# Gate and up blocks: high and low token halves as one 512-column operand in two of three accumulators

## The chip, the cores and the metric

One core of one Trainium2 chip runs the whole program. The metric is the device time of one execution in microseconds (us). The engines are TensorE (PE: matmuls, with its weight loads listed apart as PEld), VectorE (DVE), ScalarE (ACT), GpSimd (POOL) and SyncE (SP), whose queue issues most of the DMAs. PE adds its results into accumulators in PSUM, eight banks of 512 float32 columns for each of 128 partitions; everything else is in SBUF.

## The reference, cut to what matters

Two layers of an encoder with 512 tokens and 1024 channels. Each layer has a token mixer (three branches, merged by gates), a feed-forward block (FFN) and an embedding block (ple). Only the FFN's first half and the hand-overs into and out of it are touched here:

```
x = x + merged @ w_o[i]
h = rmsnorm(x, norm_ffn[i])
x = x + (silu(h @ w_ffn_gate[i]) * (h @ w_ffn_up[i])) @ w_ffn_down[i]
h = rmsnorm(x, norm_ple[i])
x = x + sigmoid(h @ w_ple_gate[i]) * (p[i] @ w_ple_in[i])
```

The FFN is 2816 wide, which is 22 blocks of 128. All values are float32.

## The kernel before

**Float32 in parts.** PE is given a rounded form of float32 (fp32r in the rows), so each operand is kept as a high part and a low part (`split`: ACT copies the high part, DVE subtracts it to get the low part). A product is three matmuls: high weights with high tokens, high weights with low tokens, low weights with high tokens. Tokens are the columns that stream; weights (128 x 128) stand.

**Gate and up.** The FFN runs over 11 steps (`gate_up`), each with two blocks of gate and two of up weights. A step doesn't take the eight half-size products of a 2 x 2 block scheme but seven, with sums of weights and sums of the two token halves (256 tokens each) as operands. Their names are a11, a12, s1, s2, s3, s4, a22. `product` (L1141) does one: 4 chunks of the contraction (`kp`) x 2 outputs `u` (gate, up) x 3 matmuls of 256 columns = 24 matmuls. The order on PE in a step is a11, a12, s2, s1, s3, s4, a22; in a layer's first step it is a11, a12, s1, s2, s3, s4, a22, begun in parts.

Three accumulators take them, one bank each: x (name ffn_sc, two buffers) gets a11, s2, s3 and a22 one on top of the other; y (ffn_tr, two buffers) gets a12; z (ffn_av, one buffer) gets s1 and then s4 on top of it. With three banks for everything else (ffn_mm), that is all eight. After each product `after(name)` reads the accumulator: a11, s2, s1 and a22 by an ACT copy into a quarter of the output, a12, s3 and s4 by a DVE add onto one. The output is two tiles g, for two blocks: half 0 and half 1 of the tokens, each with gate and up. After s4 the first tile of the step is complete, after a22 the second. `mid` then makes the operand of the second half of the FFN from a tile: DVE multiplies the gate by the row factor of the norm (wo_r), ACT takes silu, DVE multiplies by up, ACT and DVE split into high and low half. Steps alternate between two sets of output tiles (ffn_pt in even steps, ffn_y in odd ones).

**Down.** After steps 0 to 3, 4 to 7 and 8 to 10 follows `down`: eight output blocks of 8, 8 and 6 mids, in matmuls of 512 columns (L177, L178, L179 for the three parts), accumulated in ffn_mm and added to x by DVE. The last two mids of a group come last in its first two blocks.

**Order.** PE's order is the order in which the program is written. Each item (a product or a `down` block) has its weights prepared three items ahead: for a product `parted`, ACT to ffn_wh and DVE to ffn_wl, 1024 columns, three buffers each; the sums s2 and s4 are made by DVE first (ffn_rp). Loads are issued by SP some items ahead into ffn_wr, ffn_e and ffn_kh (L1041, and L1154 for `down`); sums of two loaded matrices are accumulated by DMAs issued by POOL (L1043). On ACT and DVE a scheduler orders the instructions by priority and by what it believes of their times; `follow` ties a preparation behind the latest read of an accumulator (`mark`) on the same engine. All of ACT's copies and silus are recorded at L143, all of DVE's two-operand operations at L157.

**Into and out of the FFN.** While `w_o` runs, `halves_in` and `halves_out` make the seven token operands from each chunk of the normed x. The FFN's norm is done on the way: transposes of squares into ffn_tr banks, DVE sums them, POOL takes the power (column wo_rc), and transposes broadcast it (wo_tr). At the end of `ffn` the norm for ple is begun by `main_norm`.

Of the kernel before, what the change touches and what calls it, by code (L numbers as in the profile page):

```python
# [1 line left out]

# [10 lines left out]
F32R = mybir.dt.float32r  # L13
# [7 lines left out]
P = 128  # L21
# [40 lines left out]
class Net:  # L62
    def __init__(self, nc, tc, a):
# [12 lines left out]
        self.col = self.rb = self.xin = None  # L76

# [61 lines left out]
    def ps(self, tag, shape=(P, 512), dt=F32):  # L139
        return self.psum.tile(list(shape), dt, name=self.nm(tag), tag=tag, bufs=self.pbufs[tag])  # L140
# [65 lines left out]
    def norm(self, sq, n, waits, done, spread=True, eps=None):  # L206
# [4 lines left out]
        st = self.ps("tr", (P, 4, P))  # L211
# [12 lines left out]
        bc = self.ps("tr", (P, 4, P))  # L224
# [66 lines left out]
    def build(self):  # L291
# [4 lines left out]
        self.pbufs = dict(mm=3, sc=2, tr=2, av=1)  # L296
        with tc.tile_pool(name="sb", bufs=1) as self.pool, \
# [4 lines left out]
            with tc.manual_schedule(engines={mybir.EngineType.PE}):  # L302
                h = self.opening()
                xsrc = a["xT"]
                for i in range(L):
                    h = self.layer(i, h, xsrc, xs)
                    xsrc = xs

# [129 lines left out]
    def layer(self, i, h, xsrc, xs):  # L438
# [41 lines left out]
        x, h = self.w_o(mg, xsrc, extra)  # L480
        h = self.ffn(h, x, extra)
        return self.ple(h, x, xs, self.inputs() if i == L - 1 else None)
# [506 lines left out]
    def halves_in(self, kp, x):  # L989
# [3 lines left out]
        if kp == 2:  # L993
            big = [self.sb("qk", [P, 8, 256], F32R) for _ in range(2)]
            hi, lo = [[(b[:, 0:4], 0, 4), (b[:, 4:7], 4, 7)] for b in big]
        else:
            tag = "v" if kp == 3 else "h"
            four = [self.sb(tag, [P, 4, 256], F32R) for _ in range(4)]
            hi, lo = [[(b[0], 0, 4), (b[1][:, 0:3], 4, 7)] for b in (four[0:2], four[2:4])]
# [7 lines left out]
        out = [(h[:, j], l[:, j]) for (h, a, z), (l, _, _) in zip(hi, lo) for j in range(z - a)]  # L1007
        return dict(kp=kp, bases=bases, raw=raw, other=other, hi=hi, lo=lo, out=out)

    def halves_out(self, t, x):  # L1010
# [4 lines left out]
        self.act(raw[6], x[:, 256:], AF.Copy, scale=g)  # L1015
        self.stt(raw[2], raw[3], -1.0, raw[6], ALU.mult, ALU.subtract)
        self.tt(raw[4], raw[6], t["other"], ALU.subtract)
        self.stt(raw[5], raw[2], -1.0, raw[1], ALU.mult, ALU.subtract)
        for (h, a, z), (l, _, _), b in zip(t["hi"], t["lo"], t["bases"]):
            self.split(h, l, b[:, 0:z - a])  # L1020
# [9 lines left out]
    def gate_up(self, step, ts, mids, extra):  # L1030
# [32 lines left out]
        def run(bank, name, j, kps=range(KP), first=False):  # L1063
            if bank not in out:
                out[bank] = self.ps(dict(x="sc", y="tr", z="av")[bank], (P, 2, 256))
# [527 lines left out]
```

## Time and profile before

| | us |
|---|---|
| median of three runs | 1772.5 (1772.41 to 1774.06) |
| profiled execution | 1772.31 |
| its span in the profile | 1770.5 |

| engine | busy us | share of the span | instructions |
|---|---|---|---|
| PE | 1764.0 | 100% | 10017 |
| PEld | 1550.4 | 88% | 10017 |
| DVE | 1371.0 | 77% | 2111 |
| ACT | 898.3 | 51% | 1482 |
| POOL | 63.5 | 4% | 102 |

The granted PE clock stands at full in all 40 slices, and DMA moves 145 GB/s in the mean. In the profile, instructions are named by output and inputs, with the buffer's number left out: `ffn_sc<-wo_h,ffn_wh` adds token operand wo_h times high weights ffn_wh into accumulator x. Token operands are wo_h, wo_qk and wo_v by chunk. In a timeline the row is start, length (latency, not pitch), engine, line, operation, names and shapes; brackets at the end give idle time before it and what ended that. In the chain of waits a row is start, length, and the work on the path.

### The profile page before, as it was taken

The page shows a single profiled execution, that of the slowest core. Times are in us where ns is not written, and L with a number is a line of the kernel's source. Part 1 is how long each engine was busy: PE and PEld are TensorE (multiplying, and loading weights), DVE is VectorE, ACT ScalarE, POOL GpSimd, SP SyncE. Part 2 cuts the span into 40 slices and gives each one's busy share as a digit, 9 for nine tenths or more (in the row PEclk, how much of TensorE's full clock was granted, in tenths as well). Part 3 has the DMA queues.
Part 4 walks back from the last instruction along what each step waited for, and adds up shares of the span by engine and source line. Part 5 has one row for each costly group of instructions (what it writes and reads, how often), then busy time and mean ns, then how long its engine had stood idle before and what let it go on. Part 6 is the DMA issues. An engine that isn't in the chain of part 4 may idle for free.

```text
span 1770.5 us, 26539 instructions
## 1 busy us (share of the span) xinstructions
PE 1764.0 (100%) x10017; PEld 1550.4 (88%) x10017; DVE 1371.0 (77%) x2111; ACT 898.3 (51%) x1482; POOL 63.5 (4%) x102
## 2 busy tenths in 40 slices
PE   9999999999999999999999999999999999999998
PEld 7888888888899899898888888888888998998987
DVE  7689887997877577577796788869878775775776
ACT  5566556325665255255545665563356652542544
POOL 0000000000010000000000000000000100100000
PEclk9999999999999999999999999999999999999999
DMA  5666453335656366253537574423364762763432
GB/s 194 191 191 180 126 140 84 102 99 174 196 156 178 127 167 179 85 143 118 160 122 191 177 183 122 135 84 107 105 197 139 191 191 85 187 173 111 122 111 96
DMA packets 98672, 257.51 MB, mean 145 GB/s; under 512 B 12912, under 2 KB 18160, under 8 KB 98544
## 3 DMA queue, kind: packets, MB, share of 16 engines
q1 hardware_dynamic: 91200, 231.26, 42.0%
q0 software_dynamic: 6336, 23.07, 7.4%
q8 instruction: 79, 1.29, 0.3%
q10 hardware_dynamic: 1008, 1.48, 0.2%
q14 instruction: 49, 0.40, 0.1%
HBM read 216.44 MB, written 7.86 MB: 127 GB/s over the span
## 4 chain that ended last, share of the span: by engine, by line
PE 98%; DMA 1%; DVE 0%; ACT 0%; issue 0%; ACTq 0%
PE ffn_sc L1141 14%; PE ffn_av L1141 7%; PE ffn_mm L178 4%; PE ffn_mm L179 4%; PE ffn_mm L177 4%; PE ffn_tr L1141 4%; PE mergea_mm L179 2%; PE mergea_mm L177 2%; PE mergea_mm L178 2%; PE natten_mm L177 2%; PE diff_sc L847 2%; PE gatec_mm L178 2%; PE natten_mm L178 2%; PE diff_mm L177 2%; PE diff_mm L178 2%; PE natten_mm L179 2%
## 5 line engine op out<-in xcount | busy, mean ns | idle before, releaser
L143 ACT ACTIVATE ffn_wh<-ffn_wr 128x1024 fp32r<-128x1024 f32 (+1 forms) x114 | 116.6, 1028 | 193.3 <-PE ffn_mm L178 102.0
L160 DVE SCALAR_TENSOR_TENSOR conv_z<-glu_z,pre_par,conv_z 128x512 f32<-128x512 f32 x240 | 179.2, 747 | 3.0
L157 DVE TENSOR_TENSOR ffn_wl<-ffn_wr,ffn_wh 128x1024 fp32r<-128x1024 f32 (+1 forms) x114 | 135.1, 1185 | 53.3 <-ACT ffn_wh L143 52.8
L1141 PE MATMUL ffn_sc<-wo_h,ffn_wh 128*128 128x256 f32 x704 | 130.4, 283 | 0.0
L1141 PEld LDWEIGHTS ffn_sc<-wo_h,ffn_wh 128*128 128x128 f32 x704 | 110.4, 192 | 0.8
L1141 PE MATMUL ffn_sc<-wo_h,ffn_wl 128*128 128x256 f32 x352 | 99.6, 283 | 0.0
L177 PE MATMUL ffn_mm<-ffn_z,ffn_wh 128*128 128x512 f32 x240 | 93.4, 389 | 0.0
L178 PE MATMUL ffn_mm<-ffn_z,ffn_wh 128*128 128x512 f32 x240 | 93.4, 389 | 0.0
L179 PE MATMUL ffn_mm<-ffn_z,ffn_wl 128*128 128x512 f32 x240 | 93.4, 389 | 0.0
L157 DVE TENSOR_TENSOR ffn_t<-ffn_mm,wo_r 128x512 f32<-128x512 f32 x48 | 33.1, 690 | 69.2 <-PE ffn_mm L179 69.2
L157 DVE TENSOR_TENSOR ffn_wl<-ffn_rp,ffn_wh 128x1024 fp32r<-128x1024 f32 x44 | 53.8, 1223 | 30.1 <-ACT ffn_wh L143 30.1
L143 ACT ACTIVATE mergea_wh<-mergea_wr 128x1024 fp32r<-128x1024 f32 (+1 forms) x32 | 27.1, 847 | 88.8 <-PE mergea_mm L178 80.4
L1141 PEld LDWEIGHTS ffn_sc<-wo_h,ffn_wl 128*128 128x128 f32 x352 | 67.5, 192 | 0.0
L1141 PE MATMUL ffn_sc<-wo_qk,ffn_wh 128*128 128x256 f32 x352 | 67.1, 283 | 0.0
L1141 PE MATMUL ffn_sc<-wo_v,ffn_wh 128*128 128x256 f32 x352 | 67.1, 283 | 0.0
L1141 PE MATMUL ffn_av<-wo_h,ffn_wh 128*128 128x256 f32 x352 | 65.3, 283 | 0.0
L143 ACT ACTIVATE ffn_wh<-ffn_rp 128x1024 fp32r<-128x1024 f32 x44 | 46.4, 1055 | 29.4 <-PE ffn_mm L178 17.5
L1141 PEld LDWEIGHTS ffn_sc<-wo_qk,ffn_wh 128*128 128x128 f32 x352 | 54.9, 192 | 0.0
L1141 PEld LDWEIGHTS ffn_av<-wo_h,ffn_wh 128*128 128x128 f32 x352 | 54.9, 192 | 0.0
L1141 PEld LDWEIGHTS ffn_sc<-wo_v,ffn_wh 128*128 128x128 f32 x352 | 54.9, 192 | 0.0
L179 PEld LDWEIGHTS ffn_mm<-ffn_z,ffn_wl 128*128 128x128 f32 x240 | 45.1, 188 | 9.4
L946 DVE TENSOR_REDUCE diff_s<-diff_sc 128x1 f32<-128x512 f32 x64 | 42.2, 685 | 14.3 <-PE diff_sc L847 14.3
(737 smaller groups left out, 5632.4 us busy)
## 6 DMA issues: line engine op xcount, KB each, us to landing
ffn_wr<-w_gu SPq DMA_DIRECT2D x66, 512.0 KB, 3.9
ffn_e<-w_gu SPq DMA_DIRECT2D x32, 512.0 KB, 3.4
ffn_e<-w_gu POOLq DMA_DIRECT2D x32, 512.0 KB, 8.1
ffn_wr<-w_fd SPq DMA_DIRECT2D x32, 512.0 KB, 4.3
natten_wr<-w_in SPq DMA_DIRECT2D x16, 512.0 KB, 4.2
natten_b<-bias SPq DMA_DIRECT2D x32, 256.0 KB, 4.0
gatec_wr<-w_in SPq DMA_DIRECT2D x16, 512.0 KB, 4.2
diff_wr<-w_in SPq DMA_DIRECT2D x16, 512.0 KB, 3.9
```

Of the source, the lines that this page charges most:

```text
L143: i = self.nc.scalar.activation(out, in_, func, **kw)
L157: return self.nc.vector.tensor_tensor(out, a, b, op)
L160: return self.nc.vector.scalar_tensor_tensor(out, a, s, b, op0, op1)
L177: mm(out, wh, ah, start=first, stop=False)
L178: mm(out, wh, al, start=False, stop=False)
L179: mm(out, wl, ah, start=False, stop=last)
L847: self.nc.tensor.matmul(out, st4[:, u, qs], st[:, ks], start=n == 0, stop=n == 1)
L946: nc.vector.tensor_reduce(out=m[:, u:u + 1], in_=sc, op=ALU.max, axis=AX.X, negate=True)
L1141: mm(bank[:, u], w[:, u, kp], t, start=begin and n == 0, stop=False, skip_group_check=True)
```

## The change

The products of accumulators y and z (a12 in all steps, s1 and s4 in all but a layer's first step) go to a new function `product2`. Its token operand holds the high and the low half side by side, 512 columns. One matmul takes the high weights with both, into a bank of its own for each `u`: the first 256 columns are high times high, the other 256 high times low. A second matmul of 256 columns takes the low weights with the high half, into the first 256 columns. So there are two matmuls in place of three, and the accumulator is two banks ("two", ffn_two, one buffer, taken by y and z in turn). The halves are added when they are read:

- a12: ACT copies one half into the quarter out[1,0] of the output, DVE adds the other half to out[0,0], and then DVE adds the copied quarter;
- s1: ACT copies one half negated, DVE subtracts the other;
- s4: DVE adds both, one after the other.

The first step's z has a single bank "one" as before. The three banks that ffn_tr and ffn_av had are in a pool of their own, which `part` closes and opens again around the FFN; the norm at the start of the FFN takes an mm bank for its transposes there, and `main_norm` is called after the FFN's pool is closed. The token operands are made so that halves lie side by side: for chunks other than `kp` 2 in four splits of up to two operands each, in place of two of four and three, the first two splits ahead of the sums for the later operands.

```diff
     def ps(self, tag, shape=(P, 512), dt=F32):
-        return self.psum.tile(list(shape), dt, name=self.nm(tag), tag=tag, bufs=self.pbufs[tag])
+        pool = self.psum if tag in ("mm", "sc") else self.banks
+        return pool.tile(list(shape), dt, name=self.nm(tag), tag=tag, bufs=self.pbufs[tag])
+
+    def part(self, ffn):
+
+        if self.held:
+            self.held.close()
+        self.held = ExitStack()
+        self.tag = "mm" if ffn else "tr"
+        self.banks = self.held.enter_context(
+            self.tc.tile_pool(name="bk", bufs=1, space=PSUM, reuse_waits="tile"))
...
-        self.pbufs = dict(mm=3, sc=2, tr=2, av=1)
+        self.pbufs = dict(mm=3, sc=2, tr=2, av=1, two=1, one=1)
...
         x, h = self.w_o(mg, xsrc, extra)
+        self.part(True)
         h = self.ffn(h, x, extra)
+        self.part(False)
+        self.main_norm(self.late, (3, 2))
         return self.ple(h, x, xs, self.inputs() if i == L - 1 else None)
...
-        if kp == 2:
-            big = [self.sb("qk", [P, 8, 256], F32R) for _ in range(2)]
-            hi, lo = [[(b[:, 0:4], 0, 4), (b[:, 4:7], 4, 7)] for b in big]
-        else:
-            tag = "v" if kp == 3 else "h"
-            four = [self.sb(tag, [P, 4, 256], F32R) for _ in range(4)]
-            hi, lo = [[(b[0], 0, 4), (b[1][:, 0:3], 4, 7)] for b in (four[0:2], four[2:4])]
+        n = 4 if kp == 2 else 2
+        tag = {2: "qk", 3: "v"}.get(kp, "h")
+        two = [self.sb(tag, [P, n, 2, 256], F32R) for _ in range(8 // n)]
         bases = [self.sb("z", [P, 4, 256]) for _ in range(2)]
         raw = [bases[j // 4][:, j % 4] for j in range(7)]
         other = self.sb("t", [P, 256])
@@ -1004,8 +1017,8 @@
         self.act(raw[0], x[:, 0:256], AF.Copy, scale=g)
         self.act(other, x[:, 256:], AF.Copy, scale=g)
         self.tt(raw[3], raw[0], other, ALU.subtract)
-        out = [(h[:, j], l[:, j]) for (h, a, z), (l, _, _) in zip(hi, lo) for j in range(z - a)]
-        return dict(kp=kp, bases=bases, raw=raw, other=other, hi=hi, lo=lo, out=out)
+        out = [two[j // n][:, j % n] for j in range(7)]
+        return dict(kp=kp, n=n, two=two, bases=bases, raw=raw, other=other, out=out)
...
+        n = t["n"]
+
+        def parts(js):
+            for j in range(js.start, js.stop, n):
+                c = min(n, 7 - j)
+                two = t["two"][j // n]
+                self.split(two[:, 0:c, 0], two[:, 0:c, 1], t["bases"][j // 4][:, j % 4:j % 4 + c])
+
         self.stt(raw[2], raw[3], -1.0, raw[6], ALU.mult, ALU.subtract)
+        if n == 2:
+            parts(range(0, 4))
         self.tt(raw[4], raw[6], t["other"], ALU.subtract)
         self.stt(raw[5], raw[2], -1.0, raw[1], ALU.mult, ALU.subtract)
-        for (h, a, z), (l, _, _), b in zip(t["hi"], t["lo"], t["bases"]):
-            self.split(h, l, b[:, 0:z - a])
+        parts(range(8 - 2 * n, 8))
...
         def run(bank, name, j, kps=range(KP), first=False):
+            both = bank == "y" or bank == "z" and step > 0
             if bank not in out:
-                out[bank] = self.ps(dict(x="sc", y="tr", z="av")[bank], (P, 2, 256))
-            self.product(out[bank], ops[name], ts, j, kps, first)
+                if both:
+                    out[bank] = self.ps("two", (P, 2, 2, 256))
+                else:
+                    out[bank] = self.ps("sc" if bank == "x" else "one", (P, 2, 256))
+            (self.product2 if both else self.product)(out[bank], ops[name], ts, j, kps, first)
 
         def outputs():
             g = [self.sb("y" if step % 2 else "pt", [P, 2, 512]) for _ in range(2)]
...
                 outputs()
                 self.mark["act"] = self.act(out[0, 0], out["x"], AF.Copy)
             elif name == "a12":
-                self.mark["dve"] = self.tt(out[0, 0], out[0, 0], out["y"], ALU.add)
+                y = out["y"]
+                self.mark["act"] = self.act(out[1, 0], y[:, :, 1], AF.Copy)
+                self.mark["dve"] = self.tt(out[0, 0], out[0, 0], y[:, :, 0], ALU.add)
+                self.tt(out[0, 0], out[0, 0], out[1, 0], ALU.add)
             elif name == "s2":
                 self.mark["act"] = self.act(out[0, 1], out["x"], AF.Copy)
             elif name == "s1":
-                self.mark["act"] = self.act(out[1, 1], out["z"], AF.Copy, scale=-1.0)
+                z = out["z"]
+                top = z[:, :, 0] if step else z
+                self.mark["act"] = self.act(out[1, 1], top, AF.Copy, scale=-1.0)
+                if step:
+                    self.mark["dve"] = self.tt(out[1, 1], out[1, 1], z[:, :, 1], ALU.subtract)
             elif name == "s3":
                 self.mark["dve"] = self.tt(out[1, 1], out[1, 1], out["x"], ALU.subtract)
             elif name == "s4":
-                self.mark["dve"] = self.tt(out[0, 1], out[0, 1], out["z"], ALU.add)
+                z = out["z"]
+                for part in (z[:, :, 0], z[:, :, 1]) if step else (z,):
+                    self.mark["dve"] = self.tt(out[0, 1], out[0, 1], part, ALU.add)
                 mids[2 * step] = self.mid(2 * step, out["g"][0])
...
-            th, tl = ts[kp][j]
+            th, tl = ts[kp][j][:, 0], ts[kp][j][:, 1]
...
+    def product2(self, banks, op, ts, j, kps, first):
+
+        mm = self.nc.tensor.matmul
+        hi, lo = op
+        for kp in kps:
+            both = ts[kp][j]
+            for u in range(2):
+                mm(banks[:, u], hi[:, u, kp], both, start=first and kp == 0, stop=False,
+                   skip_group_check=True)
+                mm(banks[:, u, 0], lo[:, u, kp], both[:, 0], start=False, stop=False,
+                   skip_group_check=True)
             self.chunk()
...
-        self.main_norm(st[0], (3, 2))
+        self.late = st[0]
         return hn
```

Names in the rows below: ffn_pt and ffn_y of 128x2x256 or 128x512 are output tiles of even and odd steps; ffn_tr, ffn_av and ffn_two are accumulators; ffn_wh, ffn_wl are weights in high and low part, made from ffn_wr, ffn_e or the sum ffn_rp; wo_r is the row factor; a ffn_z or ffn_y written from a tile is a mid.

DVE from the read of s4 at the end of step 2 into step 3, layer 0, before:

```order
L157 TENSOR_TENSOR ffn_pt_5374<-ffn_pt_5374,ffn_av_5448 128x2x256
L157 TENSOR_TENSOR ffn_rp_5573<-ffn_e_5181,ffn_wr_5381 128x1024
L157 TENSOR_TENSOR ffn_pt_5374<-ffn_pt_5374,wo_r_4995 128x512
L157 TENSOR_TENSOR ffn_wl_5539<-ffn_wr_5383,ffn_wh_5538 128x1024
L157 TENSOR_TENSOR ffn_pt_5374<-ffn_pt_5374 128x512
L157 TENSOR_TENSOR ffn_pt_5375<-ffn_pt_5375,wo_r_4995 128x512
L157 TENSOR_TENSOR ffn_wl_5576<-ffn_rp_5573,ffn_wh_5575 128x1024
L157 TENSOR_TENSOR ffn_z_5532<-ffn_pt_5374,ffn_z_5532 128x512
L157 TENSOR_TENSOR ffn_pt_5375<-ffn_pt_5375 128x512
L157 TENSOR_TENSOR ffn_y_5567<-ffn_pt_5375,ffn_y_5567 128x512
L157 TENSOR_TENSOR ffn_y_5604<-ffn_y_5604,ffn_tr_5613 128x2x256
```

and after:

```order
L169 TENSOR_TENSOR ffn_pt_5367<-ffn_pt_5367,ffn_two_5435 128x2x256 x2
L169 TENSOR_TENSOR ffn_wl_5512<-ffn_wr_5376,ffn_wh_5511 128x1024
L169 TENSOR_TENSOR ffn_pt_5367<-ffn_pt_5367,wo_r_5008 128x512
L169 TENSOR_TENSOR ffn_rp_5546<-ffn_e_5188,ffn_wr_5374 128x1024
L169 TENSOR_TENSOR ffn_pt_5367<-ffn_pt_5367 128x512
L169 TENSOR_TENSOR ffn_pt_5368<-ffn_pt_5368,wo_r_5008 128x512
L169 TENSOR_TENSOR ffn_wl_5549<-ffn_rp_5546,ffn_wh_5548 128x1024
L169 TENSOR_TENSOR ffn_z_5505<-ffn_pt_5367,ffn_z_5505 128x512
L169 TENSOR_TENSOR ffn_pt_5368<-ffn_pt_5368 128x512
L169 TENSOR_TENSOR ffn_y_5540<-ffn_pt_5368,ffn_y_5540 128x512
L169 TENSOR_TENSOR ffn_wl_5581<-ffn_e_5188,ffn_wh_5580 128x1024
L169 TENSOR_TENSOR ffn_y_5577<-ffn_y_5577,ffn_two_5586 128x2x256
```

The first row is two adds now, and the low half of step 3's own s1 weights has come ahead of a12's add.

ACT at the end of the first group of layer 0 (steps 0 to 3), where `down` begins; 5604 and 5605 before, and 5577 and 5578 after, are step 3's two output tiles, and the wh rows at the top are `down`'s second and third block. Before:

```order
L143 ACTIVATE ffn_wh_5778<-ffn_wr_5643 128x1024
L143 ACTIVATE ffn_y_5604<-ffn_y_5604 128x512
L143 ACTIVATE ffn_wh_5815<-ffn_wr_5676 128x1024
L143 ACTIVATE ffn_y_5772<-ffn_y_5604 128x512
L143 ACTIVATE ffn_y_5605<-ffn_sc_5579 128x2x256
L143 ACTIVATE ffn_y_5605<-ffn_y_5605 128x512
L143 ACTIVATE ffn_y_5809<-ffn_y_5605 128x512
```

and after:

```order
L155 ACTIVATE ffn_wh_5731<-ffn_wr_5610 128x1024
L155 ACTIVATE ffn_wh_5768<-ffn_wr_5643 128x1024
L155 ACTIVATE ffn_y_5577<-ffn_y_5577 128x512
L155 ACTIVATE ffn_y_5578<-ffn_sc_5552 128x2x256
L155 ACTIVATE ffn_y_5725<-ffn_y_5577 128x512
L155 ACTIVATE ffn_y_5578<-ffn_y_5578 128x512
L155 ACTIVATE ffn_y_5762<-ffn_y_5578 128x512
```

The high half of the third block's weights has changed places with the silu of step 3's first tile, and the evacuation of the second tile's last quarter with the high half of the first mid.

More of the change, by code (lines that the diff above doesn't have):

```diff
@@ L1 @@
 import math
+from contextlib import ExitStack
 import numpy as np
@@ L76, in __init__ @@
         self.col = self.rb = self.xin = None
+        self.held = None
     def run(self, gen):
@@ L210, in norm @@
         yield waits[0]
-        st = self.ps("tr", (P, 4, P))
+        st = self.ps(self.tag, (P, 4, P))
         for c in range(4):
@@ L223, in norm @@
         yield waits[1]
-        bc = self.ps("tr", (P, 4, P))
+        bc = self.ps(self.tag, (P, 4, P))
         for c in range(4):
@@ L307, in build @@
                     xsrc = xs
+                self.held.close()
     def opening(self):
@@ L480, in layer @@
         x, h = self.w_o(mg, xsrc, extra)
+        self.part(True)
         h = self.ffn(h, x, extra)
+        self.part(False)
+        self.main_norm(self.late, (3, 2))
         return self.ple(h, x, xs, self.inputs() if i == L - 1 else None)
@@ L1142, in product @@
                        skip_group_check=True)
+            self.chunk()
+    def product2(self, banks, op, ts, j, kps, first):
[8 more added lines that the diff above has]
+                   skip_group_check=True)
             self.chunk()
```

## The prediction

> **What bounds the kernel now.** I read the page's busy shares and chain first, then the stretches and the chain of an ordinary gate and up step, then single instructions where a product waits or nearly waits.
>
> ```profile
> span 1770.5 us, 26539 instructions
> PE 1764.0 (100%) x10017; PEld 1550.4 (88%) x10017; DVE 1371.0 (77%) x2111; ACT 898.3 (51%) x1482; POOL 63.5 (4%) x102
> PE 98%; DMA 1%; DVE 0%; ACT 0%; issue 0%; ACTq 0%
> ```
>
> TensorE (PE) sets the end: 98% of the chain. Its time falls only if products take less time, and every wait that the change gives it shows in full. The profiled execution took 1772.31 us, the span and 1.8 around it, and lies 0.2 under the median of 1772.5; I sum against 1772.31.
>
> ```profile
> 638.38 5.76 PE ffn_sc L1141 x48
> 644.14 2.88 PE ffn_tr L1141 x24
> 647.02 2.88 PE ffn_sc L1141 x24
> 649.90 2.88 PE ffn_av L1141 x24
> 638.40:658.50 20.10, 20.10 (x169) 20.10 (x169) 16.17 (x18) 11.49 (x16) 1.72 (x2) 1.00 0.71 170
> ```
>
> The first rows are the chain (start, length, what): 24 matmuls in 2.88 us, so one 256-column matmul each 120.0 ns (the 283 ns of a group's mean is its latency, since they overlap). The last row is the step: length, then busy us of PE, weight load, VectorE (DVE), ScalarE (ACT) and POOL, then the clock (1.00), DMA share and GB/s. DVE is busy 16.17 of 20.10: second in line.
>
> **Matmuls removed.** The price of a 512-column matmul is in `down`, just ahead of such a step:
>
> ```profile
> 619.36 0.39 PE L179 MATMUL ffn_mm<-ffn_y,ffn_wl 128*128 128x512 f32 x1
> 620.72 0.39 PE L179 MATMUL ffn_mm<-ffn_y,ffn_wl 128*128 128x512 f32 x1
> 620.95 0.40 PE L1141 MATMUL ffn_sc<-wo_h,ffn_wh 128*128 128x256 f32 x2
> 621.18 0.28 PE L1141 MATMUL ffn_sc<-wo_h,ffn_wl 128*128 128x256 f32 x1
> 576.65 0.28 PE L1141 MATMUL ffn_sc<-wo_v,ffn_wl 128*128 128x256 f32 x1
> 576.77 0.40 PE L177 MATMUL ffn_mm<-ffn_z,ffn_wh 128*128 128x512 f32 x1
> ```
>
> From the first row to the second are six matmuls (two rounds of L177, L178, L179) in 1.36 us: 226.7 ns each. A 256-column matmul behind a 512-column one costs no more (620.72 to 620.95 is 0.23, then two in 0.23), nor the other way (576.65 to 576.77 is 0.12). So two of 256 columns cost 240.0 and one of 512 costs 226.7, and each pair merged gives 13.3 ns. a12 is merged in 22 steps (11 in each of two layers), s1 and s4 in 20: 62 products with 4 x 2 pairs, 496 pairs: **-6.6 us**, -0.107 per product.
>
> "TensorE: Matmul & The Clock Gate" of the Trainium skill, section "Back-to-back issue gap", states N/2.4 + 2.5 ns for an isolated matmul at full clock. By it a pair would give only 2.5 ns, 496 pairs 1.2 us. The rows above contradict it: 120.0 and 226.7 are N/2.4 plus 13.3.
>
> **Reads added.** DVE gets 62 more 512-element operations (one per merged product), ACT 22 copies, and each layer six more splits on both engines.
>
> ```profile
> 553.93 0.69 DVE L157 TENSOR_TENSOR ffn_pt<-ffn_pt,ffn_av 128x512 f32<-128x512 f32 x1 [0.63 <-PE ffn_av L1141]
> 554.54 1.22 DVE L157 TENSOR_TENSOR ffn_rp<-ffn_e,ffn_wr 128x1024 f32<-128x1024 f32 x1
> 555.67 0.69 DVE L157 TENSOR_TENSOR ffn_pt<-ffn_pt,wo_r 128x512 f32<-128x512 f32 x1
> 559.75 0.68 DVE L157 TENSOR_TENSOR ffn_z<-ffn_pt,ffn_z 128x512 fp32r<-128x512 f32 x1
> 560.35 0.69 DVE L157 TENSOR_TENSOR ffn_pt<-ffn_pt 128x512 f32<-128x512 f32 x1
> 561.07 0.63 ACT L143 ACTIVATE ffn_y<-ffn_pt 128x512 fp32r<-128x512 f32 x1 [1.57 <-DVE ffn_pt L157]
> 561.61 0.58 ACT L143 ACTIVATE ffn_y<-ffn_sc 128x512 f32<-128x512 f32 x1
> 562.37 0.40 PE L1141 MATMUL ffn_sc<-wo_h,ffn_wh 128*128 128x256 f32 x2
> 647.50 0.68 DVE L157 TENSOR_TENSOR ffn_y<-ffn_y,ffn_tr 128x512 f32<-128x512 f32 x1
> ```
>
> Starts of DVE operations in a row lie 0.61 us apart behind 512 elements (553.93 to 554.54, out of PSUM; 559.75 to 560.35) and 1.13 behind 1024 (554.54 to 555.67). No row shows a read that takes half of each of two banks. It moves 512 elements like the first row, which reads one bank, so I take 0.60; from below that is certain enough (fewer elements are not read), and above I allow the price of 1024 elements, 1.13.
>
> In an ordinary step DVE then has 16.17 + 3 x 0.60 = 18.0 of 20.10 - 0.32 = 19.8 us: still not full. What decides is when the one two-bank tile comes free, since a12, s1 and s4 take it in turn. Between a12 and s1 lies s2. a12's add began at 647.50, and it is now behind one more operation of the same queue (s4's second add): 648.1 to 648.8. Its second add reads scratch, not the bank, and the ACT copy runs beside it. s1 begins 2.4 us after that 647.50 (649.90 in the chain, which counts by ends and lies 0.17 behind starts: 649.7), less 0.2 that PE has gained, so at 649.5: 0.65 spare with 0.05 for the semaphore. s1's tile is now read by ACT and then by a subtract on DVE; until s4 there lies s3, 2.88 us, and ahead of the subtract in DVE's queue stand at most one operation of 1.13 and one of 0.60: ACT 0.58 + 1.13 + 0.60 leaves about 0.5 spare. **0 us** in ordinary steps, up to 0.22 more per read (0.65 / 3, as three two-bank reads stand ahead of s1).
>
> **The last step of a four-step group** (steps 3 and 7 in each layer, four places) is different. There ACT makes the high half of the previous step's second mid (561.07) ahead of emptying a11's bank (561.61 to 562.19), and s2 enters that bank at 562.37: 0.18 spare, of which 0.05 goes on the semaphore (below, DVE ends at 586.99 and PE starts at 587.04). Step 7 has the same two rows:
>
> ```profile
> 686.42 0.58 ACT L143 ACTIVATE ffn_y<-ffn_sc 128x512 f32<-128x512 f32 x1
> 687.18 0.28 PE L1141 MATMUL ffn_sc<-wo_h,ffn_wh 128*128 128x256 f32 x1
> ```
>
> The high half waits for DVE (1.57 idle), and DVE has run without a gap since s4's add at 553.93. In the new order s4's second add stands behind the first at the head of that same run, 0.60 more. ACT then empties the bank at 562.79, PE can start at 562.84, and it is there 0.11 sooner than before, at 562.26: a stall of 0.58. Four times that is **+2.3 us**. In such a step s4 can also wait for s1's new subtract: between 0 and 0.3, taken 0.15: **+0.6 us**. A stalled PE comes later to all that follows in the step, so nothing else there is late by more.
>
> **The ends of groups**, where `down` needs the last mids:
>
> ```profile
> 575.54 0.64 ACT L143 ACTIVATE ffn_y<-ffn_y 128x512 f32<-128x512 f32 x1 [0.51 <-DVE ffn_y L157]
> 580.68 1.06 ACT L143 ACTIVATE ffn_wh<-ffn_wr 128x1024 fp32r<-128x1024 f32 x1 [4.51 <-DMA ffn_wr<-w_fd]
> 581.65 0.61 ACT L143 ACTIVATE ffn_y<-ffn_y 128x512 fp32r<-128x512 f32 x1
> 584.24 0.63 ACT L143 ACTIVATE ffn_y<-ffn_y 128x512 f32<-128x512 f32 x1 [1.49 <-DVE ffn_y L157]
> 585.63 0.63 ACT L143 ACTIVATE ffn_y<-ffn_y 128x512 fp32r<-128x512 f32 x1 [0.76 <-DVE ffn_y L157]
> 582.92 0.68 DVE L157 TENSOR_TENSOR ffn_y<-ffn_y,ffn_y 128x512 fp32r<-128x512 f32 x1
> 586.30 0.69 DVE L157 TENSOR_TENSOR ffn_y<-ffn_y,ffn_y 128x512 fp32r<-128x512 f32 x1 [0.70 <-ACT ffn_y L143]
> 586.32 0.49 PE L177 MATMUL ffn_mm<-ffn_y,ffn_wh 128*128 128x512 f32 x1
> 587.04 0.50 PE L178 MATMUL ffn_mm<-ffn_y,ffn_wh 128*128 128x512 f32 x1 [0.23 <-DVE ffn_y L157]
> 587.38 0.40 PE L179 MATMUL ffn_mm<-ffn_y,ffn_wl 128*128 128x512 f32 x1
> 710.39 0.69 DVE L157 TENSOR_TENSOR ffn_y<-ffn_y,ffn_y 128x512 fp32r<-128x512 f32 x1 [0.70 <-ACT ffn_y L143]
> 711.36 0.39 PE L178 MATMUL ffn_mm<-ffn_y,ffn_wh 128*128 128x512 f32 x1
> ```
>
> In layer 0's first group PE already stalls: 587.04 is 0.72 behind its L177 at 586.32, where 0.23 is usual. The cause is at 580.68: ACT waits 4.51 us for the third `down` block's weights, and the last step's second mid (evacuation, scaling, silu, product, high half, low half) runs from there to 586.99. The changed order puts that waiting instruction ahead of the first mid's silu, too, which ran at 575.54. So silu, product and both halves of the first mid now also start at 581.65 and share ACT and DVE with the second mid's chain. As that chain leaves DVE idle 0.70 at a time, its own end moves by under 0.1. But the first mid, whose low half was written by 583.60 (582.92 + 0.68), is then ready near 585.0 (silu 581.65 to 582.28, product behind the low half of the weights to 583.5, high half to 584.3, low half to 585.0), as PE comes to it. And the landing does not come sooner by what PE won in the group, so that lead is lost here. I take +0.8 there; +0.5 at the second group (low half ends 711.08, wanted at 711.36: 0.28 spare); nothing in layer 1, where no such stall stands before: **+1.3 us**. The bounds are 0, if the landing comes as much earlier as PE, and 2.5, if all four ends of four-step groups lose 0.6.
>
> **What costs nothing.** The split operands of the entry into the FFN:
>
> ```profile
> 440.00:492.00 52.00, 52.00 (x231) 43.07 (x230) 44.43 (x65) 31.34 (x49) 0.79 (x1) 1.00 0.57 182
> 505.84 0.60 PE L226 MATMUL wo_tr<-pre_ident,wo_rc 128*128 128x128 f32 x4
> 499.96 1.03 POOL L222 TENSOR_TENSOR wo_rc<-wo_sm,pre_power 128x4 f32<-128x4 f32 x1 [0.36 <-DVE wo_sm L218]
> ```
>
> DVE is busy 44.4 of 52 us there and ACT 31.3; six splits of a few tenths fit into the idle 7.6. The last splits and the norm's sum can be about 1 us later on DVE, but the norm's column, done at 501.0, is wanted only at 505.84. Without that cover it is 1 us per layer. The closing and opening of the pool, and `main_norm` behind it, put waits on PE at four places for the last readers of the old banks: at most one read's 0.60 each, taken as 0, since those readers stand before long work of PE. SP's and POOL's queues have as many instructions as before, in the same order.
>
> **Sum:** 1772.31 - 6.6 + 2.3 + 0.6 + 1.3 = 1769.9, said as **1770.0 us**.
>
> **The rivals.**
> 1. The handovers are absorbed: the landing comes earlier with PE, and the last steps don't stall since two adds of the same bank pair overlap or the run has a gap under the new order. 1772.3 - 6.6 = 1765.7, up to 1768 with one kind of stall left. For it: DVE and ACT have 3.9 and 8.6 us idle in the ordinary step. Against: the run from 553.93 has no gap. Chance 0.27.
> 2. DVE becomes the bound, slower than before: a two-bank read costs more than 0.60. Three of them (s4's two adds, a12's first) stand ahead of s1's start, so above +0.22 each s1 waits in 16 steps (all but each layer's first and the four last ones above), and the four last ones lose twice the surplus. At +0.25: 16 x 0.1 + 4 x 0.5 = 3.6, 1773.6. At +0.35 (0.95 per read): 16 x 0.4 + 4 x 0.7 = 9.2, about **1779**. At the bound of 1.13 (+0.53): 16 x 0.94 + 4 x 1.06 = 19, 1789. For it: no row reads two banks at once. Against: by the rows, a source in PSUM costs DVE no more than one in SBUF (0.69 both), and ACT less (0.58 against 0.63). Chance 0.12.
> 3. The product doesn't get cheaper: its time goes with the columns alone, which stay 3 x 256 per pair and weight, and the stalls stay: 1772.3 + 4.2 = 1776.5. The rows at 620.72 and 576.65 speak against. Chance 0.05. The rule from the Trainium skill's page above comes near this case: with its 1.2 us it would be 1775.3.
>
> My forecast (waits in the four last steps, one or two longer group ends) has 0.56, with its own range of 1768 to 1773.
>
> **How the numbers follow.** The unknown costs are 0 to 2.5 at the group ends, 0 to 1.2 at s4, and some 1 us in the first stall: 1767 to 1773. With the first rival's 1765.7 and part of the second below 1776.5 the range is **1765.5 to 1776.5**. About 0.2% (3.5 us) is what a measurement of this kernel tells from no change. Faster than that, under 1769.0: 0.25 of rival 1's 0.27 and a seventh of the forecast, 0.33. Slower, over 1776.0: most of rivals 2 and 3, 0.14. The rest, 0.53, is the same.
>
> **What would show it.** In the changed profile a merged product takes 2.77 us in the chain. Stalls of about 0.6 us stand on the first matmul of s2 in steps 3 and 7 of both layers, ended by ACT's copy out of ffn_sc. DVE's two-bank adds start 0.60 apart. In ordinary steps PE has none. Wrong it is if ordinary steps show a wait at s1 or s4 (rival 2), if a merged product still takes 2.88 us (rival 3), or if s2 of step 3 starts unhindered (rival 1).

## The result, and the profile after

The changed kernel is slower: 1784.83 us (median of 6 runs, 1780.69 to 1787.89) against 1772.45 us (1772.02 to 1774.06). The ratio is 1.0065, 95% interval 1.0054 to 1.0076. The forecast was 1770.0 with a range of 1765.5 to 1776.5, so both the sign and the size are wrong. The runs of the changed kernel also spread over 7 us, where those before spread over 2. One execution of the run "Reads alone" below took 6271.55 us and counts in none of its figures; its rows come from a profile taken again.

The profiled execution took 1785.75 us. From its page: the span, the engines, and the chain's shares by engine.

```profile
span 1784.0 us, 25685 instructions
PE 1767.1 (99%) x9521; PEld 1525.2 (85%) x9521; DVE 1409.6 (79%) x2185; ACT 910.9 (51%) x1516; POOL 63.5 (4%) x102
PE 87%; DVE 5%; DMA 4%; ACT 3%; issue 1%; ACTq 0%; SPq 0%
```

PE has 496 matmuls fewer, as the change says. But it is now only 87% of the chain (98% before): DVE, DMA and ACT have come onto it. Where, the view of waits tells (engine, line, what it waited for: us in total, times, longest):

```profile
ACT ffn_wh L155 <- DMA ffn_wr<-w_gu: 18.9, 5, 5.3
PE ffn_sc L1176 <- ACT ffn_y L155: 8.5, 4, 3.6
```

The second row is the wait that was forecast, at the four places that were forecast: s2 in steps 3 and 7 of both layers, held up by ACT's evacuation of a11's bank. The sizes are not. On PE's timeline the first and the second of the four:

```profile
563.15 0.28 PE L1189 MATMUL ffn_two<-wo_v,ffn_wl 128*128 128x256 f32 x1
563.99 0.50 PE L1176 MATMUL ffn_sc<-wo_h,ffn_wh 128*128 128x256 f32 x2 [0.56 <-ACT ffn_y L155]
...
688.76 0.28 PE L1189 MATMUL ffn_two<-wo_v,ffn_wl 128*128 128x256 f32 x1
692.60 0.50 PE L1176 MATMUL ffn_sc<-wo_h,ffn_wh 128*128 128x256 f32 x2 [3.57 <-ACT ffn_y L155]
```

Beyond the usual 0.12 us behind a 256-column matmul these are 0.72 and 3.72 us; the two of layer 1 are 1.55 and 3.16 (forecast: 0.58 each). The first row of the waits was not forecast at all: five times ACT waits for the load of a weight of gate and up. In the kernel before it never does. The chain of waits of the changed kernel ahead of the 3.72 us (start, length, what) joins the two:

```profile
670.74 0.68 DVE ffn_pt L169
...
672.48 0.68 DVE ffn_pt L169
673.16 1.15 DVE ffn_rp L169
674.31 0.02 issue
674.33 9.29 DMA ffn_wr<-w_gu
...
683.73 1.07 ACT ffn_wh L155
684.80 0.02 issue
684.82 1.23 DVE ffn_wl L169
...
690.80 0.61 DVE ffn_pt L169
691.41 0.02 issue
691.43 1.11 ACT ffn_y L155 x2
```

Read it from the top: a12's first add in step 6; a12's second add, which the change put in; s4's sum (ffn_rp), which is the last reader of a loaded a12 matrix and so frees its buffer; at once the load of step 7's a12 into that buffer, 9.29 us; ACT's high half of it; and behind that, in ACT's and DVE's queues, all that makes the previous step's mids; at last ACT's evacuation, for which s2 waits.

Before the change the same load came just in time. Its issue on SP, its row in the view of DMAs (KB, us to landing), and ACT's high half made of it:

```profile
670.64 0.33 SPq L1041 DMA_DIRECT2D ffn_wr<-w_gu  x1
```

```profile
ffn_wr<-w_gu SPq DMA_DIRECT2D x1, 512.0 KB, 7.9
```

```profile
678.69 1.06 ACT L143 ACTIVATE ffn_wh<-ffn_wr 128x1024 fp32r<-128x1024 f32 x1 [1.84 <-PE ffn_av L1141]
```

It landed at 670.64 + 7.9 = 678.5, and ACT took it at 678.69, when PE had freed the ffn_wh buffer: a spare of 0.1 to 0.2 us, in a place where the wait is put down to PE and nothing looks like a DMA limit. After the change the load is issued 3.7 us later on the clock. Of that 1.5 is PE's own lag at this place (step 6's s2 begins at 668.48, before at 667.02); at s4's read on DVE, later in the step, it is 1.75. The rows of that read, before, and after:

```profile
678.74 0.69 DVE L157 TENSOR_TENSOR ffn_pt<-ffn_pt,ffn_av 128x512 f32<-128x512 f32 x1 [0.63 <-PE ffn_av L1141]
```

```profile
680.49 1.41 DVE L169 TENSOR_TENSOR ffn_pt<-ffn_pt,ffn_two 128x512 f32<-128x512 f32 x2 [0.32 <-PE ffn_two L1189]
```

The other 2.2 are DVE's. Of these 0.6 is a12's second add. The rest stood before it: a12's first add, at 670.74 in the chain, comes 3.1 us later than a12's add in the kernel before:

```profile
667.66 0.68 DVE L157 TENSOR_TENSOR ffn_pt<-ffn_pt,ffn_tr 128x512 f32<-128x512 f32 x1
```

The load itself takes 1.4 us longer.

A second thing is not in the forecast: the clock. Stretches of the changed kernel (length; busy us of PE, weight load, DVE, ACT, POOL; granted clock; DMA share; GB/s), the waits of 3.16 and 3.72 us and the 4 us behind each, with the middle of the slow stretch:

```profile
1571.20:1574.40 3.20, 0.20 (x2) 0.00 (x0) 2.50 (x4) 1.74 (x5) 0.00 (x0) 1.00 0.37 138
1574.40:1578.40 4.00, 4.00 (x21) 4.00 (x21) 3.26 (x5) 2.33 (x3) 0.00 (x0) 0.57 0.21 40
1575.40:1577.40 2.00, 2.00 (x12) 2.00 (x11) 2.00 (x3) 1.33 (x2) 0.00 (x0) 0.50 0.00 0
...
689.00:692.60 3.60, 0.03 (x1) 0.00 (x1) 2.90 (x4) 2.14 (x5) 0.00 (x0) 1.00 0.37 137
692.60:696.60 4.00, 4.00 (x30) 3.86 (x31) 3.26 (x5) 2.93 (x4) 0.00 (x0) 1.00 0.19 50
```

After 3.0 us without a matmul the granted clock is 0.57 in the mean of 4 us, 0.50 in their middle, and a 256-column matmul takes 213 ns in place of 120: 1.5 us lost. After 3.6 us of idling at 692.60 the clock stays. The run with the matmuls in another order, below, shows the fall once more, behind an idle time of 2.7 us:

```profile
1572.28:1576.28 4.00, 4.00 (x21) 4.00 (x22) 3.26 (x5) 2.32 (x3) 0.00 (x0) 0.60 0.20 50
```

The Trainium skill's "TensorE: Matmul & The Clock Gate", section "Part 1: The HAM clock gate", has the clock fall to half after an idle window of about 3.4 us that runs freely and doesn't start anew with a kernel. That one wait cost clock and a longer one did not fits a free-running window; that 3.0 and 2.7 us sufficed does not fit its length.

**The sum again**, profile against profile (+13.4 us): merged products -3.4; the four waits of s2 9.15, with a slow restart of 0.1 behind each and the 1.5 of the clock, +11.1; the starts of `down` +3.0 (by the starts of PE's rows, layer 0's second group takes 1.3 us longer, layer 1's first 1.6, the others 0.1 or less); short waits at s1 and s4, 0.1 to 0.2 each, +1.0. Another 1.3 lies ahead of the first layer's FFN and is not put down to the change: there the profiles below differ by up to 3 us, and the latest is one of the kernel before with more buffers. Together 13.0 of the 13.4.

What the merged products give is read where nothing waits, in the last three steps of layer 0: from the first matmul of step 8 to the first of `down`, before, and after.

```profile
745.15 0.40 PE L1141 MATMUL ffn_sc<-wo_h,ffn_wh 128*128 128x256 f32 x2
...
805.63 0.40 PE L177 MATMUL ffn_mm<-ffn_z,ffn_wh 128*128 128x512 f32 x1
```

```profile
751.96 0.40 PE L1176 MATMUL ffn_sc<-wo_h,ffn_wh 128*128 128x256 f32 x2
...
811.95 0.40 PE L189 MATMUL ffn_mm<-ffn_z,ffn_wh 128*128 128x512 f32 x1
```

60.48 us before, 59.99 after, for nine merged products: 0.054 us each and 3.4 us for 62, half of the 6.6 in the forecast. With the forecast's 0.107 a product it would have been 59.52.

### The profile page after: what moved, and what is told of

It reads as the page before. It is cut to its first block, busy times and chain, and to the rows that moved or that the text cites. A ratio compares the mean times of both kernels' runs of the same rounds, so it can differ in the third digit from the quotient of the medians.

```text
span 1784.0 us, 25685 instructions
## 1 busy us (share of the span) xinstructions
PE 1767.1 (99%) x9521; PEld 1525.2 (85%) x9521; DVE 1409.6 (79%) x2185; ACT 910.9 (51%) x1516; POOL 63.5 (4%) x102
## 4 chain that ended last, share of the span: by engine, by line
PE 87%; DVE 5%; DMA 4%; ACT 3%; issue 1%; ACTq 0%; SPq 0%
PE ffn_sc L1176 9%; PE ffn_two L1187 4%; PE ffn_mm L190 4%; PE ffn_mm L191 4%; PE ffn_mm L189 4%; PE mergea_mm L189 2%; PE mergea_mm L191 2%; PE mergea_mm L190 2%; DMA ffn_wr<-w_gu 2%; PE ffn_two L1189 2%; DVE ffn_wl L169 2%; PE diff_sc L864 2%; PE gatec_mm L190 2%; PE diff_mm L190 2%; PE diff_mm L189 2%; PE gatec_mm L189 2%
## 5 line engine op out<-in xcount | busy, mean ns | idle before, releaser
L1187 PE MATMUL ffn_two<-wo_h,ffn_wh 128*128 128x512 f32 x248 | 91.0, 401 | 0.0
L1189 PE MATMUL ffn_two<-wo_h,ffn_wl 128*128 128x256 f32 x248 | 69.7, 281 | 0.0
L1187 PEld LDWEIGHTS ffn_two<-wo_h,ffn_wh 128*128 128x128 f32 x248 | 46.8, 189 | 9.4 <-DVE ffn_pt L169 0.4
```

What stands on the lines that cost most here:

```text
L1187: mm(banks[:, u], hi[:, u, kp], both, start=first and kp == 0, stop=False, skip_group_check=True)
L1189: mm(banks[:, u, 0], lo[:, u, kp], both[:, 0], start=False, stop=False, skip_group_check=True)
```

## The experiments

**Theory A**: the added adds finish s4's sum later, that frees a weight buffer later, the load lands after ACT wants it, and ACT's queue behind it is late for s2. **Theory B**, the mechanism of the forecast grown larger: the adds alone make the queues long. **Theory C**: the single two-bank buffer, or reading two banks, binds.

**Four weight buffers**, in the changed kernel and in the kernel before.

```diff
-        self.bufs = dict(wr=3, wh=3, ..., t=7, ..., sm=8, ...)
+        self.bufs = dict(wr=4, wh=3, ..., t=6, ..., sm=7, ...)
```

> The changed kernel with four buffers for loaded weights (ffn_wr) in place of three; one tag of scratch tiles has 6 in place of 7 to make room. Theory A (the added adds on DVE finish the sum s4 later, that frees a weight buffer later, the next step's a12 load is issued later and lands after ACT wants it, and ACT's queue behind it is late for s2): ACT's waits for w_gu loads (five of 3.0 to 5.3 us in the changed kernel) go, the four waits of s2 (0.7, 3.7, 1.6, 3.2 us) fall to 0.6 to 0.8 each, no half-clock stretch; about 1776 to 1778 us. Theory B (the added adds alone, in DVE's and ACT's queues, make s2 late, the load's landing only falls into the same idle time): the four waits stay, about 1785 us.

> The kernel before with the same four weight buffers, as a control for the first run. Theory A: its ACT never waits for w_gu, so nothing moves but perhaps the 0.6 us at the end of layer 0's first group: 1771.5 to 1772.5 us. Rival: the buffer is a gain by itself, whatever the change: under 1770 us.

Measured: 1772.97 us for the changed kernel (1771.99 to 1775.55, ratio 1.0003, 0.9993 to 1.0012), 1773.49 for the kernel before (ratio 1.0004, 0.9994 to 1.0013). The waits of the first:

```profile
PE ffn_sc L1176 <- ACT ffn_y L155: 2.2, 4, 0.6
```

All of ACT's waits for the FFN's loads are gone, those for `down`'s weights too, and the four waits of s2 are 0.72 us each. So the buffer alone takes back 11.9 of the 12.4 us, and the same buffer gives the kernel before nothing. Theory B falls: with the same adds the long waits are gone. Theory C falls as well, since the banks and the reads are the same. (With four buffers the scheduler puts some rows of ACT and DVE in another order; the run with one add moved, below, has no such difference on ACT.) It came out 3 to 5 us lower than expected: the starts of `down` and the waits at s1 went with the loads, and of those at s4 only 0.1 us at four places is left.

**Reads alone.** Three matmuls of 256 columns again, into the two banks; reads and the order on ACT, DVE and SP as in the changed kernel.

```diff
-            both = ts[kp][j]
+            th, tl = ts[kp][j][:, 0], ts[kp][j][:, 1]
...
-                mm(banks[:, u], hi[:, u, kp], both, start=first and kp == 0, ...)
-                mm(banks[:, u, 0], lo[:, u, kp], both[:, 0], start=False, ...)
+                for n, (w, t) in enumerate(((hi, th), (hi, tl), (lo, th))):
+                    mm(banks[:, u, n % 2], w[:, u, kp], t, start=first and kp == 0 and n == 0, ...)
```

> The changed kernel with three matmuls of 256 columns again in the merged products, written to the two banks, and all reads and their order as changed: the cost of the reads alone. The difference to the changed kernel is what merging gives on PE. By the pitch in the changed profile (355 ns for a pair, 360 for three) 496 x 5 to 7 ns: 2.5 to 3.3 us slower than the changed kernel, about 1788; by the forecast's 13.3 ns 6.6 us slower, about 1791. If theory A holds the waits of s2 stay, since the reads are the same.

> The kernel with the changed reads and three 256-column matmuls once more, for a profile at full clock (the first profile was taken on a disturbed run). Timed at 1779.3 us it was faster than the changed kernel, against the expected 1788. Theory A says why if ACT's waits for w_gu loads are fewer or shorter there: PE is 0.05 us slower in each of three products a step, so the load has more time; with them the s2 waits should be about 1 us each in place of 0.7 to 3.7.

Measured: 1778.89 us (median of four, 1778.36 to 1780.50; ratio 1.0034, 1.0020 to 1.0049). The expectation was wrong: it is not 3 us slower than the changed kernel but 5.9 faster. Its waits:

```profile
ACT ffn_wh L155 <- DMA ffn_wr<-w_gu: 11.8, 5, 2.8
PE ffn_sc L1176 <- ACT ffn_y L155: 3.1, 4, 1.2
```

Five loads are late here as well, but by 2.0 to 2.8 us in place of 3.0 to 5.3, and s2 waits 0.66 to 1.32. Merging the products took work off PE and made the kernel slower. I take the reason to be that with PE's time the loads' time shrinks too. That a lag of some tenths grows to several us from step to step I read from the rows (in layer 0 of the changed kernel ACT waits 3.03 us for a load of step 6 and 5.25 for one of step 7); no run isolates how.

**Idle adds in the kernel before.** PE and its banks untouched:

```diff
                 self.mark["dve"] = self.tt(out[0, 0], out[0, 0], out["y"], ALU.add)
+                self.tt(out[1, 0], out[0, 0], out[0, 0], ALU.add)
...
                 self.mark["dve"] = self.tt(out[0, 1], out[0, 1], out["z"], ALU.add)
+                if step:
+                    self.tt(out[1, 0], out[0, 1], out[0, 1], ALU.add)
```

> The kernel before, PE's work and its banks untouched, with two idle adds of 512 elements on DVE in every step but the first of a layer (one behind a12's add, one behind s4's add; the results are thrown away). Theory A: the added DVE time alone makes s4's sum late, ACT then waits for w_gu loads, which it never does in the kernel before, and s2 waits in steps 3 and 7; 1776 to 1782 us. Theory C (the single two-bank buffer or the two-bank read is what binds): no such waits, at most 1774 us.

Measured: 1772.62 us (ratio 1.0000, 0.9991 to 1.0009). In its waits:

```profile
ACT ffn_wh L143 <- DMA ffn_wr<-w_gu: 12.5, 5, 2.9
```

The expected 1776 to 1782 us were missed. The adds alone do make five loads late, by 2.0 to 2.9 us, as theory A has it, but no s2 waits for it and the time is that of the kernel before. (The scheduler also ordered ACT differently around these adds, so that it is not the kernel before plus adds alone.) So a late load isn't a loss by itself: lateness up to 2.9 us found cover here.

**One add moved.** a12's second add goes behind s3's read. On DVE it then stands behind s4's sum and not ahead of it; ACT's and SP's orders are the same to the row.

```diff
             elif name == "a12":
...
-                self.tt(out[0, 0], out[0, 0], out[1, 0], ALU.add)
...
             elif name == "s3":
                 self.mark["dve"] = self.tt(out[1, 1], out[1, 1], out["x"], ALU.subtract)
+                self.tt(out[0, 0], out[0, 0], out[1, 0], ALU.add)
```

> The changed kernel with a12's second add (quarter out[1,0] onto out[0,0]) put behind s3's read in place of right behind the first, so that on DVE the sum s4 stands ahead of it; nothing else moves on ACT, DVE or SP. Theory A: s4's sum ends 0.6 us sooner, the weight buffer comes free and the next a12 load is issued 0.6 us sooner, ACT's waits for w_gu loads shrink by 0.6 us or more each and the long s2 waits (3.7, 1.6, 3.2) by as much; 1779 to 1783 us. Theory B (the length of DVE's and ACT's queues alone): as many adds as before in the step, s2 waits unchanged, 1785 us.

Measured: 1773.21 us (1772.36 to 1774.40, ratio 1.0001, 0.9992 to 1.0011), with as many adds as the changed kernel. Its waits:

```profile
PE ffn_sc L1176 <- ACT ffn_y L155: 2.2, 4, 0.6
ACT ffn_wh L155 <- DMA ffn_wr<-w_gu: 2.2, 1, 2.2
```

This is the plainest evidence for theory A, and more than I expected of it: 0.6 us on one queue is worth 11.6. On DVE's timeline of this kernel, step 6:

```profile
668.27 0.68 DVE L169 TENSOR_TENSOR ffn_pt<-ffn_pt,ffn_two 128x512 f32<-128x512 f32 x1
668.87 1.22 DVE L169 TENSOR_TENSOR ffn_wl<-ffn_e,ffn_wh 128x1024 fp32r<-128x1024 f32 x1
670.01 1.22 DVE L169 TENSOR_TENSOR ffn_rp<-ffn_rp,ffn_wr 128x1024 f32<-128x1024 f32 x1
671.14 0.68 DVE L169 TENSOR_TENSOR ffn_pt<-ffn_pt,ffn_pt 128x512 f32<-128x512 f32 x1
```

The sum ends 2.96 us after the first add began (671.23), 3.56 in the changed kernel (674.30 from 670.74). The load issued then took 5.7 us here, 9.3 there. In this kernel it goes out 1.0 us ahead of POOL's accumulating load (672.21), in the changed one 0.1 behind it (674.25). With the idle adds, though, it was 0.7 behind and took 7.6; and 0.2 ahead it took 7.9 in the kernel before, but 4.9 in the run with the matmuls in another order, below. Loads of this size that start a few us earlier, without POOL's beside them, take 3 to 4 us (the one at 670.25 in the changed kernel 3.3). So the load looks slower beside POOL's; what decides how much is not settled.

**Which half of the change.** Only a12 merged, and only s1 and s4 merged (in all steps); the reads of the other half are again those of the kernel before.

```diff
-            both = bank == "y" or bank == "z" and step > 0
+            both = bank == "y"
...
```

```diff
-            both = bank == "y" or bank == "z" and step > 0
+            both = bank == "z"
...
```

> Only a12 merged; s1 and s4 as before in a single bank. 22 products in place of 62 gain 22 x 0.05 = 1.1 us. DVE's second a12 add still stands ahead of s4's sum in some steps, but s4's read is one add again: the load of the next a12 comes at most 0.6 us late. Theory A with the collision (a load issued behind POOL's accumulating DMA takes 9.3 us, ahead of it 5.7): between 1771 (no collision, no waits of s2) and 1776 (some).

> Only the second accumulator of s1 and s4 merged (in all steps), a12 as before in a single bank. 44 products gain 44 x 0.05 = 2.2 us. s4's second add still makes s2 late in steps 3 and 7 (four waits of 0.72 and 0.1 behind each: 3.3 us); nothing stands ahead of s4's sum any more, so no long waits for w_gu loads: 1772.4 - 2.2 + 3.3 = 1773.5 us. If it comes out near 1780, the adds of s4 alone make the loads late.

Measured: a12 alone 1771.83 us (ratio 0.9993, 0.9984 to 1.0002), s1 and s4 alone 1773.88 us (1.0006, 0.9997 to 1.0015). A row of the waits of each, in this order:

```profile
ACT ffn_wh L155 <- DMA ffn_wr<-w_gu: 8.2, 2, 4.6
PE ffn_sc L1174 <- ACT ffn_y L155: 2.0, 4, 0.5
```

The second has the four waits of s2, 0.67 us each, and not one late load of gate and up. The first has three late loads, these two of 3.6 and 4.6 us in step 2 of each layer and one of 1.2, and no wait of s2. So the late loads come with a12's half and the forecast's four waits with the half of s1 and s4. Neither half is slower than before by what a measurement tells; by these rows the long waits need both, a late load and an s2 that has no spare.

**The order of the matmuls.** The 512-column ones of gate and up first:

```diff
             for u in range(2):
                 mm(banks[:, u], hi[:, u, kp], both, ...)
+            for u in range(2):
                 mm(banks[:, u, 0], lo[:, u, kp], both[:, 0], ...)
```

> The changed kernel with the two 512-column matmuls of a chunk (gate, up) first and then the two of 256 columns: half as many changes from 512 to 256 columns. If the 10 ns beyond the forecast pitch lie in that change, two pairs take about 701 ns in place of 708 and PE gains 248 x 7 ns = 1.7 us; if they belong to every 512-column matmul with this operand or to the following one, the two pairs still take 708 or more and nothing is gained. Waits of s2 as in the changed kernel: 1783 or 1785 us.

Measured: 1782.93 us (1781.67 to 1785.82). The waits for loads stay, at other steps, and s2 now waits in steps 2 and 6 as well, 0.5 to 1.1 us each. What it tells of PE is again the last three steps of layer 0, without waits:

```profile
749.84 0.28 PE L1176 MATMUL ffn_sc<-wo_h,ffn_wh 128*128 128x256 f32 x1
...
809.48 0.40 PE L189 MATMUL ffn_mm<-ffn_z,ffn_wh 128*128 128x512 f32 x1
```

59.64 us, 0.35 less than the changed kernel for nine products: 62 would give 2.4 us more, 5.8 of the 6.6 forecast. Against the forecast's 59.52 the excess falls from 0.47 us to 0.12. By the starts of PE's rows a merged product without a wait takes 2.787 us here and 2.832 in the changed kernel, where 2.773 were forecast; that is 697 and 708 ns for two pairs, against 693. So about three quarters of the excess went with half of the changes between 512 and 256 columns.

**Repairs together.** The split of a step's second mid comes behind the evacuation of the next a11, so that ACT does not hold s2 up:

```diff
-            self.split(md[:, 0, :], md[:, 1, :], gate)
+            last = lambda: self.split(md[:, 0, :], md[:, 1, :], gate)
+            if f % 2 and f // 2 + 1 not in [e for _, e in PARTS] and self.rb is not None:
+                self.rest = last
+            else:
+                last()
...
                 self.mark["act"] = self.act(out[0, 0], out["x"], AF.Copy)
+                rest, self.rest = self.rest, None
+                if rest:
+                    rest()
```

With it go the order of the matmuls and the four buffers; then the late add in place of the four buffers; then all.

> The changed kernel with four ffn_wr buffers, with the 512-column matmuls of a chunk ahead of the 256-column ones, and with the split of a step's second mid put behind the evacuation of the next step's a11. By the four-buffer run (1773.0 us, four s2 waits of 0.72 us with 0.1 behind each, pairs of 355 ns): minus 3.3 us for the four waits and minus 1.7 us for 248 pairs of pairs at 701 in place of 708 to 710 ns: 1768 us, about 4.5 us under the kernel before. If the split's delay makes DVE late in turn, the waits go to s1 or s4 and it stays at 1772.

> The changed kernel with the three repairs that need no fourth buffer: a12's second add behind s3's read, the second mid's split behind the evacuation of the next a11, and the 512-column matmuls of a chunk ahead of the 256-column ones. From the run with the late add (1773.2 us): minus 3.3 us for the four s2 waits and minus 1.7 us for the order of the matmuls: 1768.2 us.

> All four repairs: four ffn_wr buffers, the late add, the late split and the order of the matmuls. With four buffers no load was late, so the late add should bring nothing more: as the run with the other three, 1766 us, within 1 us. If it is clearly lower, DVE's order mattered in itself.

Measured: 1766.08 us with four buffers (1765.90 to 1768.17, ratio 0.9963, 0.9950 to 0.9976); 1767.63 with the late add (0.9970, 0.9959 to 0.9981); 1766.31 with all (1766.05 to 1766.95, 0.9962, 0.9949 to 0.9976). From the page of the first, the engines and the chain:

```profile
PE 1757.8 (100%) x9521; PEld 1522.7 (86%) x9521; DVE 1409.5 (80%) x2185; ACT 910.7 (52%) x1516; POOL 63.5 (4%) x102
PE 98%; DMA 1%; DVE 0%; ACT 0%; issue 0%; ACTq 0%; SPq 0%
```

PE is the whole chain again. The version beats both kernels, the one before by 0.2 to 0.5%, and is some 19 us under the changed kernel with the same number of matmuls. With four buffers the late add brings nothing more; without them it comes within 1.6 us of them.

## Why the prediction was wrong, by its own steps

- **"What bounds the kernel now"**: right for the kernel before, but read too narrowly. That PE never waits says nothing of how much each of its helpers has to spare. Two engines' queues were priced; the loads that those queues release were not.
- **Matmuls removed, -6.6**: 3.4. The two neighbouring pitches were right in `down` and in the old products (120.0 and 226.7), and the boundaries quoted were single ones. Alternating them costs 354 ns a pair in place of 347. The 1.2 us that the prediction worked out from the rule in the Trainium skill's "TensorE: Matmul & The Clock Gate", section "Back-to-back issue gap", is nearer to 3.4 than the 6.6 is, but by luck: its pitches, 109.2 and 215.8 ns, are not those of the rows.
- **Reads added, "0 us in ordinary steps"**: this is the step that failed. Its spare times were taken to the moment at which a bank or a mid is wanted. The operation that came late was s4's sum, whose last read frees a weight buffer, and the load behind it had 0.1 to 0.2 us to spare. "SP's and POOL's queues have as many instructions as before, in the same order" was true and no answer: the same queue, started later, is late.
- **Four waits of s2, +2.3**: place and mechanism right; 0.72 us and a slow restart of 0.1 each where the loads are in time, 3.3 in all. Of the 0.14 by which 0.72 exceeds the forecast's 0.58, 0.12 are in the row at 680.49: s4's two adds start 0.72 apart (1.41 less the 0.69 of one), not 0.60. With the late loads 11.1, the clock's 1.5 in it. What I had said of them, that "nothing else there is late by more", was the same error.
- **s4's waits, +0.6**: about 1.0 with those at s1. **Ends of groups, +1.3**: 3.0, and nearly nothing at the first, where I put 0.8; ACT's waits for `down`'s third block are 4.4 to 6.6 us. With four buffers these waits and PE's stalls go altogether. With the late add the stalls go too, though ACT still waits 4.9 to 5.1 us there; so the late loads of gate and up have a part in them, and how is not shown.
- **The entry into the FFN at nothing**: right as far as its stretches show; no wait longer than before.
- **Rivals**: the time came out slower, where I had 0.14. The second rival named a dearer two-bank read: behind a12's first add, which is one, the next operation starts 0.60 us later, as behind a read of one bank. Only s4's pair is 0.12 dearer; whether that is the banks or that both adds go onto the same quarter, no run tells. Its sign, waits at s1 and s4 in ordinary steps, did show in step 6 of layer 0 and step 2 of layer 1, 0.1 to 0.2 us each; with four buffers, and the same reads, these are gone. So its mechanism was wrong, as was theory C.

## What to carry to other kernels

Before an operation is put into a queue with slack, look for what the operations behind it release, buffers above all, and follow those to the load that waits for them and to the time at which it lands; a spare of 0.1 or 0.2 us there is invisible in the waits, because nothing waits yet. Read a single load's landing from its own issue and not from the median of its group (here 7.9 us against 3.9). And where an added operation can't be avoided, put it behind the last reader of a loaded buffer: here that was worth 11.6 us without a single instruction less.

## What was not expected of the hardware

- The granted clock fell to 0.57 in the mean of 4 us after 3.0 us without a matmul, and stayed at 1.00 after 3.6 us elsewhere in the same run; in another run 2.7 us sufficed.
- A 512-column and a 256-column matmul in turn take 354 ns, 7 more than the pitches of each among its like; with two of each in turn about a quarter of the excess is left. What causes it is open.
- The same 512 KB load took 4.9 to 9.3 us in step 6 of the kernels here; when it starts against POOL's load, within 1 us, doesn't settle which.
- Reading halves of two banks in one DVE operation costs no more than reading one bank (a12's first add: 0.68 us long, the next operation 0.60 after its start, as in the kernel before).
